# A hybrid decoder layer on one core: order and place of the two weight parts, small lead products, and pooled sums and heads over more steps

## The chip, the cores and the metric

The kernel runs on one core of one Trainium2 chip. The metric is device time in microseconds (us) of one execution, the median of several. The core has five engines with instruction streams of their own: TensorE (PE, whose loads of stationary operands appear as PEld), VectorE (DVE), ScalarE (ACT), GpSimd (POOL) and SyncE (SP), which here only issues DMA transfers. Each engine works through its instructions in program order and waits on semaphores for the others.

## The reference

One layer on 256 tokens of width 2048, all in float32, cut to what matters:

```
h    = rms_norm(x, attn_norm_g)
proj = h @ w_in                                  # 2048 x 4096
q, k, v, p = split(proj, [1024, 2048, 3072])
q, k = rms_norm(heads(q), q_norm_g), rms_norm(heads(k), k_norm_g)   # 8 heads of 128
a = softmax(q k^T / sqrt(128) + rel_bias, causal) @ v
# pooling mixer: 4 groups of 256 channels, windows 2, 4, 8, 16
m = concat_g((window_sum_g(p_g) / count_g - p_g) @ pool_w[g]) * pool_scale
x = x + concat(a, m) @ w_out                     # 2048 x 2048
u = rms_norm(x, ffn_norm_g) @ w_up               # 2048 x 11264
y = conv_b + causal depthwise convolution of u, width 3
gate, val = split(y, 2)
x = x + (silu(gate) * val) @ w_down              # 5632 x 2048
```

The block-sparse selection of the attention has one block of 256 tokens here, so that it is plain causal attention.

## The kernel before

**Two parts for one float32.** TensorE multiplies in a format of fewer bits (fp32r). So each weight and each activation is split into a high part, the rounded value, and a low part, the rest. A product is the sum of three: high by high, low weight by high activation, high weight by low activation. ScalarE writes the high part of a weight chunk `wh` (L115, a copy with rounding), VectorE the low part `wl` (L116, raw minus high).

**Chunks and steps.** The weights come as 88 chunks of 128 x 2048 floats in the order of use. A step is half a chunk, 1024 columns; there are 176. SP loads chunk after chunk into four raw buffers; `release` issues the next load as soon as a raw buffer has been split. `wh` and `wl` have three buffers each, rows of 2048 + 64 floats, and the chunk begins some floats into the row: `WOFF` gives that offset for high and low, one pair for the first 24 chunks and one for all others. The tiles of the activations (`xh`, `cat`, `x2h`, `hid`) hold per row, for each of 16 blocks of channels, 256 tokens of the high part and then 256 of the low part.

**The two kinds of product.** In the first 48 steps the activations are the stationary operand (loaded, 128 x 128) and 512 columns of weights stream past it: the v projection (L152, 16 steps, accumulated in four 512-column banks) and the q and k projections (L162, four blocks of eight steps, in the order k, q, k, q, four heads each). In all later steps the weights are loaded and the activations stream. There `feat_mm` issues two products per block of 128 x 128 weights: `wl` with the 256 columns of the high activations (L169), then `wh` with all 512 columns, high and low (L171). Both add into a 512-column bank of PSUM, whose two halves are added up when the block is done (`add_halves`, ScalarE L400 and VectorE L401). Two places use `feat_sum` (L178), with three products of 256 columns and no sum behind: the products of the pooling mixer (`pool_half`) and the last down block.

**The order of the steps.** v (steps 0 to 15); k, q, k, q (16 to 47); the pooling mixer's projection for g = 3, 2, 1, 0 (48 to 63, four steps each); the output projection, eight blocks of 256 output channels (four steps each, with two steps of `pool_half` among those of the first); then three times: a stretch of the gate and value blocks in turn, and eight down blocks. What the other engines do in between is set by hand: `after(u, f)` hangs f behind step u, and the loop at the end (L655 to L666) runs, for each step: the split of the chunk that is used two chunks later (at even steps), what was deferred, the products of the step, and the hooks. So a hook's place in each engine's stream is fixed by its step.

**Attention.** When a q or k block is done, `head_norm` normalises it by head (VectorE writes `qn` or `kn`), and two steps later `head_T` transposes it on TensorE (L338). Per head, `scores` multiplies, adds the bias, finds the row maxima and writes their negatives (`mx`, L358) on VectorE and takes the exponential on ScalarE (L360); `normalise` (one step later) takes the reciprocal of the sums and scales `e` on VectorE (L365, L367); `probs_T` (three steps later) transposes `e` on TensorE (L374); `head_out` (five steps later) multiplies by v (L384) and splits the result into `cat` (L390). A head starts every second step. The rows of the relative bias are written out to DRAM (`band`) and read back shifted as `T`, by the queue of POOL, once for each four heads.

**The pooling mixer.** Behind the last step of a group, `pool_window` adds the halves, scales (L407), sums the window by doubling (L411, one addition of 128 x 512 for each power of two: four for the window of 16, one for the window of 2), takes the mean (L413) and subtracts the input (L414). Two steps later (at once for g = 0) `pool_mixed` splits the result into `cat`.

**Behind an output block**, `residual` adds x and sums the squares for the second norm, and `x2_split` splits two blocks of channels into `x2h`, for the gate and value blocks. `stats2` (two steps into the first gate block) forms the row sums on TensorE (L281) for the scale that `gate` and `value` apply.

The lines that set pace and order:

```
WOFF = ((24, 24), (8, 24))
...
for n, (ws, k) in enumerate(ks):
    nc.tensor.matmul(ps[:, S:], wl[:, ws], act[:, k, 0, :], start=(first and n == 0), ...)
    nc.tensor.matmul(ps, wh[:, ws], act[:, k, :, :], start=False, ...)
...
after(u, lambda h=h, b=b: scores(h, st["qT", b], st["kT", b], st["T", b]))
after(u + 1, lambda h=h: normalise(h))
after(u + 3, lambda h=h: probs_T(h))
after(u + 5, lambda h=h: head_out(h))
```

Of the kernel before, what the change touches and what calls it, by code (L numbers as in the profile page):

```python
# [34 lines left out]
NH = 8  # L35
# [16 lines left out]
WOFF = ((24, 24), (8, 24))  # L52
# [19 lines left out]
def layer(ctx: ExitStack, tc: tile.TileContext, xT, wts, par, relT, ident_d, onehot_d, icnt_d, out):  # L72
# [27 lines left out]
    def load(c, pieces=1, j=0, queue=None):  # L100

        if c not in raws:
            raws[c] = wpool.tile([P, CH], F32, name="raw", tag="raw", bufs=RAWS)
        s = slice(j * CH // pieces, (j + 1) * CH // pieces)
        (queue or nc.sync).dma_start(raws[c][:, s], wts[c][:, s])
# [35 lines left out]
    def val_half(u, ps):  # L141
# [5 lines left out]
        for b in (0, 1) if u < KT - 2 else (u - KT + 2,):  # L147
            for k, (wh, wl) in zip(ks, parts):
                for t in range(NT):
                    ws, ts = slice(b * 512, (b + 1) * 512), slice(t * P, (t + 1) * P)  # L150
                    for n, (a, w) in enumerate(((0, wh), (0, wl), (1, wh))):
                        nc.tensor.matmul(ps[b][:, t, :], xh[:, k, a, ts], w[:, ws],  # L152
                                         start=(k == 0 and n == 0), stop=(k == KT - 1 and n == 2))
# [12 lines left out]
    def feat_mm(ps, wh, wl, act, ks, first, last):  # L166

        for n, (ws, k) in enumerate(ks):
            nc.tensor.matmul(ps[:, S:], wl[:, ws], act[:, k, 0, :],  # L169
                             start=(first and n == 0), stop=False, skip_group_check=True)  # L170
            nc.tensor.matmul(ps, wh[:, ws], act[:, k, :, :], start=False,  # L171
# [46 lines left out]
    load(0, 4, 0, nc.scalar)  # L218
    nc.scalar.preload_act_table_set("natural_log_exp_and_others")
    load_xT(0, 1)  # L220
    load(0, 4, 1)
    load_xT(1, 2)
    load(0, 2, 1)
    for c in range(1, RAWS):
        load_xT(2 * c, 2 * c + 2)
        load(c, 2, 0)
        load(c, 2, 1)
    x_first()
    split_piece(0, 0, 512)
    split_piece(0, 512, 512)  # L230
# [6 lines left out]
    rsb = early.tile([NH, L], F32, name="rsb", tag="e", bufs=2)  # L237
# [108 lines left out]
    def scores(h, qT, kT, T):  # L346
# [6 lines left out]
        e = early.tile([P, L], F32, name="e", tag="e", bufs=2)  # L353
        mx = early.tile([P, 4], F32, name="mx", tag="mx", bufs=2)
# [48 lines left out]
    def pool_window(ps, g):  # L403
        s = early.tile([P, 2, S], F32, name="pst", tag=("sq", "hn")[g % 2])
        eng = nc.vector
        add_halves(s, ps)
        eng.tensor_tensor(pa[0][:, :, PAD:], s, rrow[:, None, :].to_broadcast([P, 2, S]), op=OP.mult)  # L407
        cur, d, i = pa[0], 1, 1
        while d < WINDOWS[g]:
            nxt = pa[i]  # L410
            eng.tensor_tensor(nxt[:, :, PAD:], cur[:, :, PAD:], cur[:, :, PAD - d:PAD + S - d], op=OP.add)  # L411
            cur, d, i = nxt, 2 * d, 3 - i
        eng.tensor_tensor(s, cur[:, :, PAD:], icnt[:, g:g + 1, :].to_broadcast([P, 2, S]), op=OP.mult)  # L413
        eng.tensor_tensor(s, s, pa[0][:, :, PAD:], op=OP.subtract)  # L414
        st["win", g] = s

# [316 lines left out]
```

## Time and profile before

| | us |
|---|---|
| runs: median of 3 (lowest, highest) | 1054.22 (1051.92, 1055.24) |
| the profiled execution, its own time | 1056.07 |
| its span, first to last instruction | 1054.3 |
| TensorE busy | 1036.8 (98%) |
| loads of its stationary operands | 900.1 (85%) |
| VectorE busy | 703.6 (67%) |
| ScalarE busy | 508.7 (48%) |

The profile's page comes from one execution with the hardware profiler. The span leaves out what lies before the first and behind the last instruction. Busy times are sums over an engine's instructions. TensorE's products overlap in its pipeline, and their ends are modelled, so the length of a product in a row is longer than the step to the next one; the pace has to be read from starts. The mean clock granted to TensorE over the span was 0.994 of full speed. The DMA engines moved 200.42 MB at 190 GB/s in the mean, and the main queue (the weights) kept them busy for 52.5% of the span.

By stretches, from the view of windows (us from the start of the span; busy times of the engines; TensorE's clock):

| stretch | steps in it | TensorE | VectorE | ScalarE | clock |
|---|---|---|---|---|---|
| 0 to 58 | v | 54.97 | 37.15 | 34.87 | 1.00 |
| 58 to 172 | k, q, k, q with the first heads | 109.52 | 61.77 | 48.95 | 0.97 |
| 172 to 214 | pooling mixer with the last heads | 37.39 | 33.41 | 18.12 | 0.96 |
| 214 to 324 | output projection | 108.47 | 76.45 | 58.39 | 1.00 |
| 324 to 1054 | gate, value, down | 726.41 | 494.84 | 348.36 | 1.00 |

In rows of the timeline the first column is the start and the second the length (of several instructions, from the first's start to the last's end); what stands in brackets is the idle time of the engine before the row and what ended it. In rows of the windows the columns are: the window, its length, busy time and count of PE, PEld, DVE, ACT and POOL, TensorE's granted clock, the share of the DMA engines, and GB/s.

### The profile page before, as it was taken

Reading aid. Unit: us, or ns where it says so; the run is one execution under the profiler, and the core shown is the slowest. Engines: PE = TensorE matmul, PEld = TensorE weight load, DVE = VectorE, ACT = ScalarE, POOL = GpSimd, SP = SyncE. Lnnn points to the kernel's source line nnn. Section 1 sums busy time; section 2 is a strip of 40 time slices with the busy share of each in tenths; the row PEclk is TensorE's granted clock in tenths of the full one; section 3 lists DMA queues with packets and bytes.
Section 4 is the critical chain, followed back from the end, with each engine's and each line's share of the span. In section 5 each row is a group of like instructions: output and inputs, shape, how many; then the busy total and the mean of one; then the engine's idle time right before and its main releaser. Section 6 shows DMA issues by size and latency. Waiting matters only on the chain.

```text
span 1054.3 us, 13723 instructions
## 1 busy us (share of the span) xinstructions
PE 1036.8 (98%) x5786; PEld 900.1 (85%) x5786; DVE 703.6 (67%) x755; ACT 508.7 (48%) x526; POOL 3.7 (0%) x13
## 2 busy tenths in 40 slices
PE   8999989899999999999999999999999999999998
PEld 7877778798887888888888888888888888888887
DVE  6654647786766777777655577776765557777763
ACT  7534543545545455455443454555543445555441
POOL 0000000000000000000000000000000000000000
PEclk9999989999999999999999999999999999999999
DMA  9677533456463555545555555455455554554551
GB/s 358 252 186 225 207 140 122 142 221 234 170 220 136 197 197 175 204 181 200 200 190 174 196 186 196 178 197 202 165 198 196 200 184 176 200 200 163 205 192 40
DMA packets 31102, 200.42 MB, mean 190 GB/s; under 512 B 3784, under 2 KB 4584, under 8 KB 8256
## 3 DMA queue, kind: packets, MB, share of 16 engines
q1 hardware_dynamic: 29904, 196.66, 52.5%
q0 software_dynamic: 992, 2.63, 1.5%
q8 instruction: 45, 0.74, 0.3%
q10 hardware_dynamic: 144, 0.26, 0.1%
q14 instruction: 17, 0.14, 0.0%
HBM read 195.86 MB, written 3.67 MB: 189 GB/s over the span
## 4 chain that ended last, share of the span: by engine, by line
PE 83%; DVE 3%; ACT 2%; issue 1%; ACTq 0%; DVEq 0%
PE ps_feat L171 53%; PE ps_feat L169 27%; PE ps_tok L162 2%; DVE wl L116 1%; PE ps_feat L178 1%; ACT wh L115 1%; ACT e L360 1%; PE ps_pool L178 1%; DVE pa L411 0%; PE ps_T L338 0%; DVE e L356 0%; PE ps_av L384 0%; DVE pst L413 0%; DVE pst L401 0%; DVE pa L407 0%
## 5 line engine op out<-in xcount | busy, mean ns | idle before, releaser
L116 DVE TENSOR_TENSOR wl<-raw,wh 128x2048 fp32r<-128x2048 f32 (+2 forms) x186 | 415.5, 2234 | 218.3 <-ACT wh L115 215.8
L171 PE MATMUL ps_feat<-x2h,wh 128*128 128x512 f32 x1408 | 489.8, 393 | 0.0
L115 ACT ACTIVATE wh<-raw 128x2048 fp32r<-128x2048 f32 (+2 forms) x186 | 346.7, 1864 | 102.2 <-PE ps_feat L171 61.9
L169 PE MATMUL ps_feat<-x2h,wl 128*128 128x256 f32 x1408 | 392.3, 279 | 0.0
L171 PEld LDWEIGHTS ps_feat<-x2h,wh 128*128 128x128 f32 x1408 | 264.9, 188 | 59.9
L169 PEld LDWEIGHTS ps_feat<-x2h,wl 128*128 128x128 f32 x1408 | 265.0, 188 | 0.0
L171 PE MATMUL ps_feat<-hid,wh 128*128 128x512 f32 x680 | 235.9, 392 | 0.0
L169 PE MATMUL ps_feat<-hid,wl 128*128 128x256 f32 x680 | 189.0, 278 | 0.0
L171 PEld LDWEIGHTS ps_feat<-hid,wh 128*128 128x128 f32 x680 | 127.6, 188 | 28.8
L169 PEld LDWEIGHTS ps_feat<-hid,wl 128*128 128x128 f32 x680 | 127.6, 188 | 0.0
L400 ACT ACTIVATE fs<-ps_feat 128x512 f32<-128x512 f32 x75 | 44.8, 597 | 170.8 <-PE ps_feat L171 170.8
L401 DVE TENSOR_TENSOR fs<-ps_feat,fs 128x512 f32<-128x512 f32 x75 | 51.7, 689 | 57.5 <-ACT fs L400 57.5
L171 PE MATMUL ps_feat<-cat,wh 128*128 128x512 f32 x256 | 88.9, 391 | 0.0
L162 PE MATMUL ps_tok<-wh,xh 128*128 128x512 f32 x256 | 85.5, 407 | 0.0
L169 PE MATMUL ps_feat<-cat,wl 128*128 128x256 f32 x256 | 71.5, 279 | 0.0
L162 PEld LDWEIGHTS ps_tok<-wh,xh 128*128 128x128 f32 x256 | 49.1, 192 | 11.8 <-issue 0.4
L171 PEld LDWEIGHTS ps_feat<-cat,wh 128*128 128x128 f32 x256 | 48.1, 188 | 10.5
L624 ACT ACTIVATE hid<-y 128x512 fp32r<-128x512 f32 x22 | 13.9, 633 | 86.7 <-DVE y L623 86.7
L162 PE MATMUL ps_tok<-wl,xh 128*128 128x512 f32 x128 | 51.4, 401 | 0.0
L169 PEld LDWEIGHTS ps_feat<-cat,wl 128*128 128x128 f32 x256 | 47.9, 187 | 0.2 <-DVE wl L116 0.2
L599 ACT ACTIVATE y<-u,pv 128x256 f32<-128x256 f32 x88 | 47.8, 591 | 0.0
L611 ACT ACTIVATE y<-y 128x512 f32<-128x512 f32 x22 | 13.9, 634 | 68.1 <-DVE y L602 68.1
(111 smaller groups left out, 680.9 us busy)
## 6 DMA issues: line engine op xcount, KB each, us to landing
raw<-in_wts SPq DMA_DIRECT2D x177, 1024.0 KB, 4.8
raw<-in_wts SPq DMA_DIRECT2D x7, 512.0 KB, 8.0
x<-in_xT SPq DMA_DIRECT2D x1, 2048.0 KB, 10.7
xboth<-in_xT SPq DMA_DIRECT2D x7, 256.0 KB, 8.7
out<-x SPq DMA_DIRECT2D x7, 256.0 KB, 3.3
band<-rsb POOLq DMA_DIRECT2D x1, 1536.0 KB, 35.1
T<-band POOLq DMA_DIRECT2D x2, 512.0 KB, 7.1
icnt<-in_icnt SPq DMA_DIRECT2D x1, 512.0 KB, 6.0
```

Of the source, the lines that this page charges most:

```text
L115: nc.scalar.activation(wh, w, AF.Copy)
L116: nc.vector.tensor_tensor(wl, w, wh.bitcast(F32), op=OP.subtract)
L162: nc.tensor.matmul(ps[:, t, :], act[:, k0 + k, a, ts], w[:, ws], start=(first and k == 0 and n == 0), stop=(last and k == 1 and n == 2))
L169: nc.tensor.matmul(ps[:, S:], wl[:, ws], act[:, k, 0, :], start=(first and n == 0), stop=False, skip_group_check=True)
L171: nc.tensor.matmul(ps, wh[:, ws], act[:, k, :, :], start=False, stop=(last and n == len(ks) - 1), skip_group_check=True)
L178: nc.tensor.matmul(ps, w[:, ws], act[:, k, a, :], start=(first and n == 0 and i == 0), stop=(last and n == len(ks) - 1 and i == 2))
L360: nc.scalar.activation(e[:, s], e[:, s], AF.Exp, bias=mx[:, t:t + 1], accum_out=mx[:, 2 + t:3 + t])
L400: nc.scalar.activation(dst, ps[:, :, S:], AF.Copy)
L401: nc.vector.tensor_tensor(dst, ps[:, :, :S], dst, op=OP.add)
L599: nc.scalar.activation(y[:, m, :], u[:, m, 2:], AF.Identity, scale=cw[2], bias=col(C_CB + f))
L611: nc.scalar.activation(y, y, AF.Silu)
L624: nc.scalar.activation(hid[:, ks, 0, :], y, AF.Copy)
```

## The change

**WOFF.** From chunk 24 on the low part begins 28 floats into its row instead of 24 (112 bytes instead of 96); the high part stays at 8 floats (32 bytes).

**feat_mm** issues the product of `wh` (512 columns) first and that of `wl` (256 columns) behind it.

**A lead product** of 16 columns, with `wh` loaded and 16 columns of `wl` streaming, into the first bank of a block, which the block's first product then overwrites. It stands ahead of seven blocks: the output block g = 1, and in each third the first gate block and the first down block.

**The first chunk** is loaded, split and used in pieces of 256, 256 and 512 columns (`FIRST`) instead of 512 and 512 in its first half; `load` takes a start and a length.

**Heads.** `head_T` moves from two to three steps behind its block; the heads start four steps behind the end of their q block instead of three, with `normalise` one step, `probs_T` four and `head_out` six steps behind `scores`. `e` and `mx` have three buffers instead of two. The second `T` is fetched at `at + 8`, with `at` one step later.

**Pooled sums.** `pool_window` keeps the sum of the halves and the scaling. `window_sums` does two of the doublings behind the same step, and two more with the mean (`window_mean`) one step later; `pool_mixed` stays two steps later. For g = 0 all stays behind the last step.

**x2_split** of the last output block moves from a hook behind the first gate step into the end of the block's own last step.

```diff
-WOFF = ((24, 24), (8, 24))
+WOFF = ((24, 24), (8, 28))
...
-        for b in (0, 1) if u < KT - 2 else (u - KT + 2,):
+        if u == 0:
+            pieces = FIRST
+        else:
+            pieces = ((0, 512), (512, 512)) if u < KT - 2 else (((u - KT + 2) * 512, 512),)
+        for lo, cols in pieces:
...
         for n, (ws, k) in enumerate(ks):
-            nc.tensor.matmul(ps[:, S:], wl[:, ws], act[:, k, 0, :],
+            nc.tensor.matmul(ps, wh[:, ws], act[:, k, :, :],
                              start=(first and n == 0), stop=False, skip_group_check=True)
-            nc.tensor.matmul(ps, wh[:, ws], act[:, k, :, :], start=False,
+            nc.tensor.matmul(ps[:, S:], wl[:, ws], act[:, k, 0, :], start=False,
                              stop=(last and n == len(ks) - 1), skip_group_check=True)
...
-    load(0, 4, 0, nc.scalar)
+    FIRST = ((0, 256), (256, 256), (512, 512))
+    load(0, *FIRST[0], queue=nc.scalar)
     nc.scalar.preload_act_table_set("natural_log_exp_and_others")
     load_xT(0, 1)
-    load(0, 4, 1)
+    for piece in FIRST[1:]:
+        load(0, *piece)
     load_xT(1, 2)
-    load(0, 2, 1)
+    load(0, HALF, HALF)
...
-        e = early.tile([P, L], F32, name="e", tag="e", bufs=2)
-        mx = early.tile([P, 4], F32, name="mx", tag="mx", bufs=2)
+        e = early.tile([P, L], F32, name="e", tag="e", bufs=3)
+        mx = early.tile([P, 4], F32, name="mx", tag="mx", bufs=3)
...
+    def window_sums(g, d, n):
+
+        for _ in range(n):
+            if d == WINDOWS[g]:
+                return
+            i = d.bit_length()
+            cur, nxt = pa[0 if d == 1 else 1 + i % 2], pa[1 + (i + 1) % 2]
+            nc.vector.tensor_tensor(nxt[:, :, PAD:], cur[:, :, PAD:], cur[:, :, PAD - d:PAD + S - d], op=OP.add)
+            d *= 2
+
+    def window_mean(g):
+        s = st["win", g]
+        cur = pa[1 + WINDOWS[g].bit_length() % 2]
+        nc.vector.tensor_tensor(s, cur[:, :, PAD:], icnt[:, g:g + 1, :].to_broadcast([P, 2, S]), op=OP.mult)
+        nc.vector.tensor_tensor(s, s, pa[0][:, :, PAD:], op=OP.subtract)
...
+                    if lead:
+                        wh, wl = wparts[u // 2]
+                        o = (u % 2) * HALF
+                        nc.tensor.matmul(box["ps"][0][:, :16], wh[:, o:o + P], wl[:, o:o + 16], start=True, stop=True)
...
-        after(len(steps) + (2 if g else 0), lambda g=g: pool_mixed(g))
+        e = len(steps)
+        if g:
+            after(e, lambda g=g: window_sums(g, 1, 2))
+            after(e + 1, lambda g=g: (window_sums(g, 4, 2), window_mean(g)))
+            after(e + 2, lambda g=g: pool_mixed(g))
+        else:
+            after(e, lambda g=g: (window_sums(g, 1, 1), window_mean(g), pool_mixed(g)))
...
-            after(st[nm, b, "end"] + 2, lambda nm=nm, b=b, gc=gc: st.__setitem__(
+            after(st[nm, b, "end"] + 3, lambda nm=nm, b=b, gc=gc: st.__setitem__(
                 (nm + "T", b), head_T(st[nm, b], gc, nm + "T")))
-        at = st["q", b, "end"] + 3
+        at = st["q", b, "end"] + 4
...
-            after(u + 3, lambda h=h: probs_T(h))
-            after(u + 5, lambda h=h: head_out(h))
+            after(u + 4, lambda h=h: probs_T(h))
+            after(u + 6, lambda h=h: head_out(h))
         if b == 0:
-            after(at + 7, lambda: st.__setitem__(("T", 1), bias_tile(4)))
+            after(at + 8, lambda: st.__setitem__(("T", 1), bias_tile(4)))
...
+        def post(ps, g=g):
+            residual(ps, g)
+            if g == D // 256 - 1:
+                x2_split(g)
+        steps += feat_block(lambda: st["cat"], OK, post, lead=(g == 1))
+        if g < D // 256 - 1:
+            after(len(steps) + (2 if g == 0 else 0), lambda g=g: x2_split(g))
...
+            steps += feat_block(lambda: late["h"], XK, lambda ps, g=g: gate(ps, g), lead=(g == g0))
...
+                                     lambda ps, g=g, n=n, final=final: down(ps, g, n == 2, final), final,
+                                     lead=(g == 0)))
```

TensorE at the border between the last output block (streaming `cat`) and the first gate block (streaming `x2h`), before:

```order
L171 MATMUL ps_feat<-cat,wh 128x512
L169 MATMUL ps_feat<-cat,wl 128x256
L171 MATMUL ps_feat<-cat,wh 128x512
L169 MATMUL ps_feat<-x2h,wl 128x256
L171 MATMUL ps_feat<-x2h,wh 128x512
L169 MATMUL ps_feat<-x2h,wl 128x256
```

and now:

```order
L177 MATMUL ps_feat<-cat,wl 128x256
L175 MATMUL ps_feat<-cat,wh 128x512
L177 MATMUL ps_feat<-cat,wl 128x256
L489 MATMUL ps_feat<-wl,wh 128x16
L175 MATMUL ps_feat<-x2h,wh 128x512
L177 MATMUL ps_feat<-x2h,wl 128x256
```

Low and high have changed places in each pair, and the lead product L489 stands between the blocks. Loads and products still alternate: the load of the `wl` of L177 runs beside the 512 columns of L175, that of the next `wh` beside the 256 columns of L177.

VectorE at the second of the last four heads (in the first pooling group; L356 finds the row maxima, `mx` holds their negatives), before:

```order
L356 ISA e,mx<-ps_s,T 128x128
L356 ISA mx 128x1
L356 ISA e,mx<-ps_s,T 128x256
L356 ISA mx 128x1
L358 TENSOR_SCALAR mx<-mx 128x2
L365 RECIPROCAL mx<-mx 128x2
L367 SCALAR_TENSOR_TENSOR e<-e,mx,rrow 128x128
L367 SCALAR_TENSOR_TENSOR e<-e,mx,rrow 128x256
L116 TENSOR_TENSOR wl<-raw,wh 128x2048
```

and now (L364 is the L356 of before, L366 the L358, L373 and L375 the L365 and L367, L438 `pool_mixed`):

```order
L364 ISA e,mx<-ps_s,T 128x128
L364 ISA mx 128x1
L364 ISA e,mx<-ps_s,T 128x256
L364 ISA mx 128x1
L366 TENSOR_SCALAR mx<-mx 128x2
L116 TENSOR_TENSOR wl<-raw,wh 128x2048
L438 TENSOR_TENSOR cat<-pst,cat 128x2x256
L373 RECIPROCAL mx<-mx 128x2
L375 SCALAR_TENSOR_TENSOR e<-e,mx,rrow 128x128
L375 SCALAR_TENSOR_TENSOR e<-e,mx,rrow 128x256
```

The heads have moved by one step, so that the split of the next chunk, which runs at even steps, now stands between the maxima and the normalisation instead of behind it; the mixer's split L438 follows it there.

More of the change, by code (lines that the diff above doesn't have):

```diff
@@ L98, in layer, with load @@
     raws, wparts = {}, {}
-    def load(c, pieces=1, j=0, queue=None):
+    def load(c, lo=0, n=CH, queue=None):
         if c not in raws:
             raws[c] = wpool.tile([P, CH], F32, name="raw", tag="raw", bufs=RAWS)
-        s = slice(j * CH // pieces, (j + 1) * CH // pieces)
+        s = slice(lo, lo + n)
         (queue or nc.sync).dma_start(raws[c][:, s], wts[c][:, s])
@@ L216, in x_first @@
         nc.vector.scalar_tensor_tensor(lo, xin[:, 0, :], xboth[:, :1], hi.bitcast(F32), op0=OP.mult, op1=OP.subtract)
-    load(0, 4, 0, nc.scalar)
+    FIRST = ((0, 256), (256, 256), (512, 512))
+    load(0, *FIRST[0], queue=nc.scalar)
     nc.scalar.preload_act_table_set("natural_log_exp_and_others")
     load_xT(0, 1)
-    load(0, 4, 1)
+    for piece in FIRST[1:]:
+        load(0, *piece)
     load_xT(1, 2)
-    load(0, 2, 1)
+    load(0, HALF, HALF)
     for c in range(1, RAWS):
         load_xT(2 * c, 2 * c + 2)
-        load(c, 2, 0)
-        load(c, 2, 1)
+        load(c, 0, HALF)
+        load(c, HALF, HALF)
     x_first()
-    split_piece(0, 0, 512)
-    split_piece(0, 512, 512)
+    for piece in FIRST:
+        split_piece(0, *piece)
     for k in range(1, AHEAD):
@@ L236, in layer @@
     onehot = early.tile([32, 2 * S], F32, name="onehot", tag="T")
-    rsb = early.tile([NH, L], F32, name="rsb", tag="e", bufs=2)
+    rsb = early.tile([NH, L], F32, name="rsb", tag="e", bufs=3)
     icnt = early.tile([P, 4, S], F32, name="icnt")
@@ L460, in tok_block, with feat_block @@
             steps.append([run])
-    def feat_block(act, ks, post, final=False):
+    def feat_block(act, ks, post, final=False, lead=False):
         box, runs = {}, []
@@ L574, in layer @@
     for g in range(D // 256):
-        steps += feat_block(lambda: st["cat"], OK, lambda ps, g=g: residual(ps, g))
-        after(len(steps) + (2 if g == 0 else 0), lambda g=g: x2_split(g))
+        def post(ps, g=g):
[5 more added lines that the diff above has]
+            after(len(steps) + (2 if g == 0 else 0), lambda g=g: x2_split(g))
         if g == 0:
@@ L641, in layer @@
         for g in range(g0, g1):
-            steps += feat_block(lambda: late["h"], XK, lambda ps, g=g: gate(ps, g))
+            steps += feat_block(lambda: late["h"], XK, lambda ps, g=g: gate(ps, g), lead=(g == g0))
             steps += feat_block(lambda: late["h"], XK, lambda ps, g=g, j=g - g0: value(ps, g, j))
```

19 lines of the change are left out of this document (6 added, 13 removed).

## The prediction

> **What bounds the kernel now.** I read the page's busy times first, then TensorE's own waits, then its timeline. The page gives TensorE 98% of the span, and its waits are few:
>
> ```profile
> PE 1036.8 (98%) x5786; PEld 900.1 (85%) x5786; DVE 703.6 (67%) x755; ACT 508.7 (48%) x526; POOL 3.7 (0%) x13
> ...
> PE ps_av L384 <- DVE mx L365: 3.1, 1, 3.1
> PE ps_T L338 <- DVE cat L390: 3.0, 1, 3.0
> PE ps_row L281 <- issue: 2.0, 1, 2.0
> PE ps_T L338 <- DVE qn L329: 1.5, 1, 1.5
> PE ps_eT L374 <- DVE e L367: 1.5, 1, 1.5
> ```
>
> The timeline gives the places of the first, the last of attention's, and the one of L281 (the bracket holds the idle time before):
>
> ```profile
> 107.04 1.09 PE L338 MATMUL ps_T<-ident,qn 128*128 128x128 f32 x8 [1.47 <-DVE qn L329]
> 198.24 0.67 PE L384 MATMUL ps_av<-eT,v 128*128 128x256 f32 x2 [3.08 <-DVE mx L365]
> 324.47 0.67 PE L281 MATMUL ps_row<-sq,ones 128*128 128x256 f32 x2 [2.00 <-issue]
> ```
>
> Four of the five stand between 105 and 198 us, where attention and the pooling mixer share VectorE. The list of waits holds none that ends behind 324 us. Behind three of the waits the windows show TensorE at half clock:
>
> ```profile
> 137.40:144.30 6.90, 5.90 (x18) 5.04 (x19) 2.19 (x5) 3.77 (x6) 0.04 (x1) 0.51 0.57 217
> 198.90:202.30 3.40, 3.40 (x15) 3.01 (x14) 2.97 (x7) 0.30 (x1) 0.00 (x0) 0.50 0.14 19
> 325.20:328.60 3.40, 3.40 (x12) 2.89 (x11) 1.68 (x4) 0.83 (x2) 0.00 (x0) 0.50 0.81 306
> ```
>
> Half of the work time in them is lost: about 2.9 (5.90 / 2), 1.7 and 1.7 us. So 11.1 us of waits and 6.3 us of half clock can be had from scheduling, 17.4 us in all. Everything else is the pace of the products, and this is its size:
>
> ```profile
> L171 PE MATMUL ps_feat<-x2h,wh 128*128 128x512 f32 x1408 | 489.8, 393 | 0.0
> L171 PE MATMUL ps_feat<-hid,wh 128*128 128x512 f32 x680 | 235.9, 392 | 0.0
> L171 PE MATMUL ps_feat<-cat,wh 128*128 128x512 f32 x256 | 88.9, 391 | 0.0
> ```
>
> Each of these high products has a low one of 256 columns (L169) beside it: 1408 + 680 + 256 = 2344 pairs. The timeline shows their pace at full clock, and at half clock (326 us):
>
> ```profile
> 340.08 0.28 PE L169 MATMUL ps_feat<-x2h,wl 128*128 128x256 f32 x1
> 340.19 0.39 PE L171 MATMUL ps_feat<-x2h,wh 128*128 128x512 f32 x1
> 340.42 0.28 PE L169 MATMUL ps_feat<-x2h,wl 128*128 128x256 f32 x1
> ...
> 326.10 0.41 PE L169 MATMUL ps_feat<-x2h,wl 128*128 128x256 f32 x1
> 326.31 0.63 PE L171 MATMUL ps_feat<-x2h,wh 128*128 128x512 f32 x1
> 326.74 0.41 PE L169 MATMUL ps_feat<-x2h,wl 128*128 128x256 f32 x1
> ```
>
> The first column is the start, so what counts is the step from row to row. A more exact period comes from ScalarE, which repeats its split once per gate and value block (64 pairs):
>
> ```profile
> 348.49 1.90 ACT L115 ACTIVATE wh<-raw 128x2048 fp32r<-128x2048 f32 x1
> 481.61 1.90 ACT L115 ACTIVATE wh<-raw 128x2048 fp32r<-128x2048 f32 x1
> ```
>
> Six such blocks, 384 pairs, take 133.12 us: 346.7 ns per pair, so 2344 pairs are 812.6 us of the 1054. At half clock the pair takes 0.64 us, and half of that is 320 ns. At full clock 26.7 ns are lost in each pair, 13.3 per product, though nobody is waited for. Two other stages, of equal products, show what the loss can be:
>
> ```profile
> 73.98 0.63 PE L162 MATMUL ps_tok<-wh,xh 128*128 128x512 f32 x2
> 74.45 0.40 PE L162 MATMUL ps_tok<-wl,xh 128*128 128x512 f32 x1
> 74.68 0.63 PE L162 MATMUL ps_tok<-wh,xh 128*128 128x512 f32 x2
> ...
> 222.14 0.40 PE L178 MATMUL ps_pool<-cat,wh 128*128 128x256 f32 x2
> 222.38 0.28 PE L178 MATMUL ps_pool<-cat,wl 128*128 128x256 f32 x1
> 222.50 0.40 PE L178 MATMUL ps_pool<-cat,wh 128*128 128x256 f32 x2
> ```
>
> L162: three products of 512 columns in 0.70 us, 233.3 each against 213.3 by the half clock: 20.0 lost. L178: three of 256 in 0.36 us, 120.0 against 106.7: 13.3 lost. So the loss comes in units of 6.7 ns: two per product where the columns stream from the activations (L178, L171 with L169), three where they stream from the weights (L162). If length alone set it, a 512 with a 256 would lose 33.3; it loses 26.7. What differs is which row of SBUF is loaded while which is streamed.
>
> **The change part by part.** *Low part moved by 16 bytes (WOFF).* In the code each piece that is loaded or streamed starts a multiple of 512 bytes into its row, so one offset fixes the relation between a load and the columns streaming past it for all 2344 pairs. So far the offsets are 96 and 32 bytes; the low part's load, which runs beside the 512 columns of L171, goes to 112, an odd multiple of 16. No row shows an odd one, so the price is bounded by the losses above: at best the low load costs nothing, −13.3 ns × 2344 = −31.3 us; at worst it takes a unit more, as in L162, +6.7 × 2344 = +15.6 us. I take one unit less, −15.6 us: the loss moves in units, the offset moves by the smallest step that can change the relation, and L162 against L178 (one unit apart) is the nearest pair of rows.
>
> The Trainium skill speaks against it: TensorE: Matmul & The Clock Gate, Step-by-step: what each phase is for, says that loads and streamed columns have independent SBUF read ports, so that loading the next weights takes nothing from the running product. By it this term is 0 wherever the weights lie. The trace agrees only at half clock; at full clock 13.3 to 20.0 ns per product are lost.
>
> *High part first (L171 before L169).* Loads and products alternate as before, so the steady pace has no term. At a block's start the low part is needed one product later; TensorE waits for no low part after 11 us, so nothing is won.
>
> *The 16-column products.* Seven more loads and products on a TensorE that is never idle there. The nearest row has one column:
>
> ```profile
> 57.91 0.50 PE L301 MATMUL ps_col<-ones,xboth 128*128 128x1 f32 x4
> 58.27 0.68 PE L281 MATMUL ps_row<-xboth,ones 128*128 128x256 f32 x2
> ```
>
> Four in 0.36 us are 0.09 each; with L178's 0.12 as the other end, 7 × 0.1 = +0.7 us (0.6 to 0.8).
>
> *Smaller first pieces.* TensorE's second half step and SP's issues set the pace at the start:
>
> ```profile
> 8.07 1.06 ACT L115 ACTIVATE wh<-raw 128x1024 fp32r<-128x1024 f32 x1 [1.50 <-DMA raw<-in_wts]
> 10.45 0.50 PE L152 MATMUL ps_val<-wl,xh 128*128 128x512 f32 x1 [0.76 <-DVE wl L116]
> ...
> 3.07 1.17 SPq L105 DMA_DIRECT2D raw<-in_wts  x2
> ```
>
> That half is a transfer that the change puts one SP issue further back (two take 1.17 us, one 0.6). The first product comes earlier, but the wait at 10.45 absorbs it: 0 to +0.6, taken as +0.1.
>
> *Heads one step later, pooled sums over three steps.* A step is some 2.8 us (12 × 0.233, 8 × 0.347). The wait for qn (1.5) should go, since 2.8 is more than 1.5. The others hang on VectorE, and there the new order costs something. One head, now:
>
> ```profile
> 184.05 0.17 DVE L358 TENSOR_SCALAR mx<-mx 128x2 f32<-128x2 f32 x1
> 185.28 0.17 DVE L365 RECIPROCAL mx<-mx 128x2 f32<-128x2 f32 x1 [1.05 <-ACT e L360]
> 185.48 0.75 DVE L367 SCALAR_TENSOR_TENSOR e<-e,mx,rrow 128x128 f32<-128x128 f32 x2
> 187.46 2.29 DVE L116 TENSOR_TENSOR wl<-raw,wh 128x2048 fp32r<-128x2048 f32 x1 [1.23 <-ACT wh L115]
> ...
> 185.52 1.91 ACT L115 ACTIVATE wh<-raw 128x2048 fp32r<-128x2048 f32 x1
> ...
> 172.00:214.00 42.00, 37.39 (x209) 32.36 (x209) 33.41 (x64) 18.12 (x33) 0.00 (x0) 0.96 0.36 127
> ```
>
> After mx VectorE waits 1.05 for ScalarE's exponentials, normalises, and waits 1.23 for the high split: 2.3 us idle. In the new order the low split stands right behind mx; its high split on ScalarE still follows the exponentials (about 1.0, then 1.9), so VectorE idles 2.9 us in one stretch and normalises afterwards. Behind the waiting split stand the window sums and the normalisation, and TensorE's transposes wait for those. In 172 to 214 us VectorE works 33.4 of 42; with four heads at 2.9 us of waiting it would need 45.0, up to 3 us more than now. Against it: the wait of 1.5 goes, and the 3.0 before ps_T shrinks by 2.8, less 0.6 × 3 heads. That is −1.5 − 1.0 + 3 = about 0; the ends are −13.7 (the four waits' 9.1 and two half-clock windows' 4.6 all gone) and +5 (0.6 for each of eight heads). The T load (POOL queue) moves with its step and keeps eight steps of cover, and the third e buffer keeps a later head off one still to be transposed.
>
> *x2_split of the last group.* It passes one split on ScalarE and VectorE, but the sum L570, for which ps_row waits, still stands behind the same two low splits. 0; the 2.0 us and their half clock stay.
>
> Sum: −15.6 + 0.7 + 0.1 + 0 = −14.8 us. The profiled execution took 1056.07 us, 1.77 outside its span of 1054.3; it would take 1041.3. It lies 1.85 above the median of the runs shown (1054.22), and for that median the sum gives **1039 us**.
>
> **The rivals.**
> *The 16 bytes do nothing* (an independent port, or a loss that hangs on the count of loads alone). For it: L178 loses the same 13.3 per product as L171 with L169, though there the loads beside one product come from the high and the low tile in turn. Against it: L162. Time: 1054.2 + 0.8 = 1055, with the attention stage's ends 1041 to 1060.
> *The low load then costs nothing*: 1054.2 − 31.3 + 0.8 = 1024.
> *One unit more* (slower): the odd line meets the 512 streamed columns as the loads of L162 do, +15.6 + 0.8: 1071. It decides from about 0.35 ns per pair on, since 2344 pairs make 0.8 us of that; for it speaks that offsets of this kind lose three units in one stage already.
>
> **How the numbers follow.** One unit less 0.42 (1031 to 1047 with the attention stage's play); free 0.13; nothing 0.30; one unit more 0.15. A measurement of this kernel tells some 0.3% (3.2 us) from no change. Of the case "nothing" I put 0.20 within that, 0.06 faster through the stage, 0.04 slower: faster 0.42 + 0.13 + 0.06 = 0.61, same 0.20, slower 0.15 + 0.04 = 0.19. The range 1021 to 1058 holds the first, most of the free case and the third, about 0.82; it leaves out the last.
>
> **What would show it.** Right: 64 pairs in 21.76 us instead of 22.19 (340.0 ns a pair), steady to the end, L171's step near 223. Wrong in the main term: the period still at 346.7, or at 353.3. For the stage: waits before 224 us of some 7 to 12 us in all, VectorE waiting 2.9 us behind each mx, the qn wait gone, ps_row's 2.0 still there. The prediction fails altogether if the pace changes between stages, since I let one pace hold for all 2344 pairs.

## The result and the profile after

The changed kernel takes **1062.9 us** (median of 4 runs, 1062.08 to 1063.29) against 1054.47 before: ratio 1.0083, interval 1.0065 to 1.0101. It is slower by 0.8%, where 1.4% faster was forecast, and lies above the forecast's range. The profiled execution took 1063.29 us with a span of 1061.5, 7.2 more than before.

Two counts have to be put right first: the kernel has 181 chunks and 362 steps, not 88 and 176, and 2472 pairs of products, since the 128 pairs of the pooling projection (L171 with `xh`) were left out of the 2344.

The page's busy times and TensorE's waits (total, times, longest), after:

```profile
PE 1042.3 (98%) x5799; PEld 901.3 (85%) x5799; DVE 702.7 (66%) x756; ACT 507.7 (48%) x527; POOL 3.7 (0%) x13
...
PE ps_av L392 <- DVE cat L398: 4.2, 2, 3.5
PE ps_val L157 <- ACT wh L115: 2.1, 1, 2.1
PE ps_s L359 <- DVE mx L364: 2.0, 2, 1.2
PE ps_T L346 <- DVE cat L398: 2.0, 1, 2.0
PE ps_row L289 <- issue: 1.9, 1, 1.9
```

Where the time went, by the starts of each stage's first product in the two traces (us):

| stretch | before | after | difference |
|---|---|---|---|
| to the end of v | 52.31 | 56.58 | +4.27 |
| k, q, k, q | 108.14 | 103.70 | −4.44 |
| pooling projection | 58.92 | 60.87 | +1.96 |
| output projection | 94.62 | 96.62 | +2.00 |
| gate, value, down (to the end of the span) | 740.3 | 743.7 | +3.4 |

**The start.** The timeline of TensorE and ScalarE and the windows of the first microseconds, after (columns as before):

```profile
11.05 0.79 PE L157 MATMUL ps_val<-wh,xh 128*128 128x512 f32 x1 [2.15 <-ACT wh L115]
...
9.94 1.06 ACT L115 ACTIVATE wh<-raw 128x1024 fp32r<-128x1024 f32 x1 [2.40 <-DMA raw<-in_wts]
...
4.00:5.00 1.00, 0.86 (x5) 0.49 (x4) 0.96 (x3) 0.72 (x2) 0.00 (x0) 1.00 0.66 197
5.00:6.00 1.00, 0.76 (x7) 0.74 (x7) 0.54 (x2) 0.00 (x0) 0.00 (x0) 1.00 0.70 208
...
10.70:17.55 6.85, 6.04 (x13) 4.42 (x14) 5.58 (x7) 5.50 (x9) 0.00 (x0) 0.51 1.03 413
```

and the same two windows before:

```profile
4.00:5.00 1.00, 0.64 (x4) 0.45 (x3) 0.28 (x1) 0.12 (x1) 0.00 (x0) 1.00 1.00 339
5.00:6.00 1.00, 0.43 (x1) 0.19 (x1) 0.96 (x3) 0.97 (x2) 0.00 (x0) 1.00 1.07 327
```

With the smaller pieces the transfers run at 197 and 208 GB/s where they ran at 339 and 327. The second half of the first chunk is there for its split at 9.94 us instead of 8.07; TensorE waits for 2.15 us, and then runs at a clock of 0.51 for 6.85 us, in which half of its 6.04 us of work, about 3.0 us, is lost.

**The pace.** ScalarE's splits 12 chunks (192 pairs) apart, in the second gate and value stretch, after:

```profile
600.43 1.91 ACT L115 ACTIVATE wh<-raw 128x2048 fp32r<-128x2048 f32 x1
667.42 1.91 ACT L115 ACTIVATE wh<-raw 128x2048 fp32r<-128x2048 f32 x1
```

66.99 / 192 = 348.9 ns a pair, 2.2 more than before, and it is so from the first pair to the last. The starts of the high products stand 346, 349 and 352 ns apart in turn (rounded, 1046.67 in three pairs), where before they stood evenly 346.67 apart. 2472 x 2.22 = 5.5 us.

**The pooling mixer.** VectorE at one head, and two of TensorE's waits, after:

```profile
186.12 0.17 DVE L366 TENSOR_SCALAR mx<-mx 128x2 f32<-128x2 f32 x1
189.16 2.29 DVE L116 TENSOR_TENSOR wl<-raw,wh 128x2048 fp32r<-128x2048 f32 x1 [2.86 <-ACT wh L115]
191.36 0.68 DVE L438 TENSOR_TENSOR cat<-pst,cat 128x512 fp32r<-128x512 f32 x1
191.97 0.16 DVE L373 RECIPROCAL mx<-mx 128x2 f32<-128x2 f32 x1
...
194.84 0.92 PE L359 MATMUL ps_s<-kT,qT 128*128 128x128 f32 x4 [1.21 <-DVE mx L364]
204.87 0.70 PE L392 MATMUL ps_av<-eT,v 128*128 128x256 f32 x2 [3.52 <-DVE cat L398]
```

VectorE waits for 2.9 us behind the maxima, as forecast, and the chain behind it reaches TensorE's products of the next head (1.21) and of `head_out` (3.52).

### The profile page after: what moved, and what is told of

Read it like the earlier page. It is cut to its first block, busy times and chain, and to the rows that moved or that the text cites. A ratio compares the mean times of both kernels' runs of the same rounds, so it can differ in the third digit from the quotient of the medians.

```text
span 1061.5 us, 13820 instructions
## 1 busy us (share of the span) xinstructions
PE 1042.3 (98%) x5799; PEld 901.3 (85%) x5799; DVE 702.7 (66%) x756; ACT 507.7 (48%) x527; POOL 3.7 (0%) x13
## 4 chain that ended last, share of the span: by engine, by line
PE 86%; DVE 5%; DMA 4%; ACT 3%; issue 1%; SPq 0%; ACTq 0%; DVEq 0%
PE ps_feat L175 51%; PE ps_feat L177 26%; PE ps_val L157 4%; PE ps_tok L168 3%; DMA raw<-in_wts 3%; DVE wl L116 3%; ACT wh L115 2%; DMA x<-in_xT 1%; PE ps_feat L184 1%; ACT e L368 1%; DVE e L375 0%; DVE pa L425 0%; DVE e L364 0%; PE ps_av L392 0%; DVE pst L431 0%
## 5 line engine op out<-in xcount | busy, mean ns | idle before, releaser
L175 PE MATMUL ps_feat<-x2h,wh 128*128 128x512 f32 x1408 | 491.8, 393 | 0.0
L177 PE MATMUL ps_feat<-x2h,wl 128*128 128x256 f32 x1408 | 393.3, 279 | 0.0
L175 PEld LDWEIGHTS ps_feat<-x2h,wh 128*128 128x128 f32 x1408 | 264.6, 188 | 61.3
L177 PEld LDWEIGHTS ps_feat<-x2h,wl 128*128 128x128 f32 x1408 | 264.0, 187 | 0.0
L175 PE MATMUL ps_feat<-hid,wh 128*128 128x512 f32 x680 | 237.6, 393 | 0.0
L177 PE MATMUL ps_feat<-hid,wl 128*128 128x256 f32 x680 | 189.9, 279 | 0.0
L175 PEld LDWEIGHTS ps_feat<-hid,wh 128*128 128x128 f32 x680 | 127.8, 188 | 29.6
L177 PEld LDWEIGHTS ps_feat<-hid,wl 128*128 128x128 f32 x680 | 127.5, 187 | 0.0
L409 DVE TENSOR_TENSOR fs<-ps_feat,fs 128x512 f32<-128x512 f32 x75 | 51.6, 689 | 60.9 <-ACT fs L408 60.9
L175 PE MATMUL ps_feat<-cat,wh 128*128 128x512 f32 x256 | 89.9, 394 | 0.0
L177 PE MATMUL ps_feat<-cat,wl 128*128 128x256 f32 x256 | 71.6, 280 | 0.7 <-DVE wl L116 0.7
L175 PEld LDWEIGHTS ps_feat<-cat,wh 128*128 128x128 f32 x256 | 48.1, 188 | 11.3 <-DVE cat L462 0.3
L177 PEld LDWEIGHTS ps_feat<-cat,wl 128*128 128x128 f32 x256 | 48.0, 187 | 1.0 <-DVE wl L116 1.0
L175 PE MATMUL ps_feat<-xh,wh 128*128 128x512 f32 x128 | 47.2, 409 | 0.0
```

Source lines behind the costliest of these rows:

```text
L175: nc.tensor.matmul(ps, wh[:, ws], act[:, k, :, :], start=(first and n == 0), stop=False, skip_group_check=True)
L409: nc.vector.tensor_tensor(dst, ps[:, :, :S], dst, op=OP.add)
```

## The experiments

Ratios are to the kernel before on the same chip, intervals 95%. A place (16, 4) means the high part at 16 floats and the low part at 4. Executions at that place fall into two groups more than 20 us apart, so all times are given where both groups occur.

### The first pieces

```diff
-    FIRST = ((0, 256), (256, 256), (512, 512))
+    FIRST = ((0, 512), (512, 512))
```

> The changed kernel with the first half chunk loaded, split and used in two pieces of 512 columns, as before. In the changed kernel TensorE waits 2.15 us at 8.9 us for the high split of the second half step, and runs at half clock from 10.7 to 17.6 us; the v stage takes 51.95 us instead of 46.75, though it starts 0.93 earlier. Theory A (the smaller transfers slow the loads behind them, the wait grows past the point where the clock is halved): the wait falls back to under 1 us, no half clock, v stage near 46.8, the run 4.3 us faster than the changed kernel, near 1058.6. Theory B (half clock at the start comes by chance from execution to execution, whatever the pieces): v stage still 50 to 52, the run near 1062.9.

1060.6 us (5 runs), ratio 1.0054 (1.0042 to 1.0066): 2.3 less than the changed kernel by the medians, and about 3 by the two ratios, each to the kernel before on its own chip. TensorE's waits at the start of its timeline:

```profile
5.70 0.50 PE L157 MATMUL ps_val<-wh,xh 128*128 128x512 f32 x1 [1.09 <-ACT wh L115]
10.29 0.50 PE L157 MATMUL ps_val<-wl,xh 128*128 128x512 f32 x1 [0.76 <-DVE wl L116]
```

The wait of 2.15 and the half clock are gone, and v takes 46.47 instead of 51.95: theory A, by mechanism. The 4.3 forecast did not come in full: in this execution the half clock stands behind the wait for the row sums again (325 to 328.5 us, 1.7 lost), where the profiled execution of the changed kernel had none. Nor do the pieces decide alone: both profiled executions with the smaller pieces have half clock at the start, but so has one of the 18 with the old ones (the run with fifteen leads below, 3.4 us of it behind waits of 0.89 and 0.76 us). In the other run with the smaller pieces (place undone) the transfers ran at 236 and 274 GB/s and the wait was 1.55 us, so the size of this loss differs between executions.

### Place alone, place undone

```diff
-WOFF = ((24, 24), (8, 24))          # kernel before
+WOFF = ((24, 24), (8, 28))
```

> The kernel before with the low part at 28 floats instead of 24, and nothing else. In the changed kernel the pair takes 348.9 ns instead of 346.7. Theory O (the place of the low part sets the pace): 348.9 ns a pair here, and 2472 x 2.2 ns = 5.4 us more than before, near 1059.9. Theory R (high first sets the pace): 346.7 ns, near 1054.5. Theory L (the lead products put the pairs out of step): 346.7 ns, 1054.5.

```diff
-WOFF = ((24, 24), (8, 28))          # changed kernel
+WOFF = ((24, 24), (8, 24))
```

> The changed kernel with the low part back at 24 floats. Theory O: 346.7 ns a pair, 5.4 us faster than the changed kernel, near 1057.5. Theories R and L: 348.9 ns, near 1062.9. If place and order act only together, both this and the offset alone run at 346.7.

The place alone: 1059.56 us, ratio 1.0044 (1.0030 to 1.0059). ScalarE's splits 192 pairs apart:

```profile
603.98 1.90 ACT L115 ACTIVATE wh<-raw 128x2048 fp32r<-128x2048 f32 x1
670.97 1.90 ACT L115 ACTIVATE wh<-raw 128x2048 fp32r<-128x2048 f32 x1
```

66.99 again: 348.9. Undone in the changed kernel: 1058.95 us, ratio 1.0037 (1.0024 to 1.0050), 4.0 less than the changed kernel by the medians, and 4.9 by the ratios. Its splits 192 pairs apart:

```profile
603.90 1.90 ACT L115 ACTIVATE wh<-raw 128x2048 fp32r<-128x2048 f32 x1
670.47 1.90 ACT L115 ACTIVATE wh<-raw 128x2048 fp32r<-128x2048 f32 x1
```

66.57 / 192 = 346.7 ns a pair. Theory O; the place does it alone.

The kernel with the place undone, at the old pace, has the seven leads. A down block stretch with one lead in it takes 88.86 us instead of 88.75: 0.11 a lead, 0.8 us for all seven.

### Order alone, schedule alone

The kernel before with the two products of `feat_mm` exchanged, as in the change:

> The kernel before with the high product first in each pair, and nothing else. Theory O: 346.7 ns a pair, no change, 1055. Theory R: 348.9 ns or another period, 1058 to 1060 or more.

1055.46 us (11 runs), ratio 1.0004 (0.9995 to 1.0013), 346.67 ns a pair. The order costs nothing and brings nothing by itself.

The changed kernel with everything but the schedule taken back:

```diff
-WOFF = ((24, 24), (8, 28))
+WOFF = ((24, 24), (8, 24))
...
-    FIRST = ((0, 256), (256, 256), (512, 512))
+    FIRST = ((0, 512), (512, 512))
...
-                    if lead:
+                    if False:
```

and the low product first again.

> The changed kernel with the old places (8, 24), low first, no lead products and the old first pieces: what is left are the heads one step later, the pooled sums over more steps, and the last split of x2h in its block's own step. Theory S (the stage as read off the changed kernel): the waits of 1.5 and 1.1 before the transposes go, the half clock of 3.4 us lost at 137 us goes or moves, and VectorE's longer waits in the pooling mixer add 2 to 3.5 us: 1 to 4 us less than before, 1051 to 1054. Theory Z (the sum in the prediction): about 0, 1054 to 1056. If the half clock only moves, 1055 to 1057.

1055.33 us (11 runs), ratio 1.0005 (0.9995 to 1.0015): theory Z. The four q and k blocks take 3.7 us less than before, the pooling and output projections 3.8 more. Part of the 3.7 is half clock and not the schedule: the profiled execution before has 6.83 us of it at 137 us, this one 3.41, and in the run with the order alone, with none there, these blocks take 105.67 us against 104.44 here. What the transposes gain is given back where VectorE is late. The pooling projection takes 60.9 us in this run, with 6.83 us of half clock, and in that of the old first pieces, with none, where TensorE waits 2.29 us more for `head_out` (at 209.66 us): VectorE, and not TensorE's clock, sets its length. In the output projection TensorE waits 1.34 us at 247 us for a low part, where before it has no such wait.

### Two scans of the place

The kernel before, from chunk 49 on (gate, value, down) with another place for every four chunks; in the second scan with high first and another shuffle:

```diff
-            offs = WOFF[0 if c < TOK_CHUNKS else 1]
+            offs = WOFF[0 if c < TOK_CHUNKS else 1] if c < 49 else SCAN[(c - 49) // 4]
```

> The kernel before, with another place of the two parts for every four chunks (64 pairs, some 22 us) from the gate and value stage on: 32 places, high part at 0, 8, 16 or 24 floats, low part at 0, 4, 8 to 28, in a shuffled order. Same work. Theory O: the pair's period differs from place to place in units that repeat, with (8, 24) at 346.7 and (8, 28) at 348.9, and some places lower, down to 320 if a free one exists. Theory N (a loss of 13.3 ns per product belongs to the load itself, wherever it lies): 346 to 349 at every place, in no relation to the offsets.

> The kernel before with the high product first in each pair, and the same 32 places of the two parts as in the first scan, four chunks each, in another shuffled order. Theory O (place alone sets the pace): the same period at the same place as in the first scan: 340.0 at high 16, low 4; 346.7 at (8, 24); 348.9 at (8, 28); 353.3 at (8, 16), (16, 16) and (24, 16). Theory H (the pace is a phase into which TensorE falls after a change, and keeps): other periods at the same places, and 340.0 elsewhere or nowhere. Theory R (order and place act together): the table is another one, but a steady one.

The period in ns, from the starts of the high products in the trace, some 45 pairs for each place; where the scans differ by over 0.1, first / second. The stretches with TensorE's wait for the row sums in them ((24, 8) in the first scan, (24, 16) in the second) ran at 353.3 on both sides of the wait:

| high \ low | 0 | 4 | 8 | 12 | 16 | 20 | 24 | 28 |
|---|---|---|---|---|---|---|---|---|
| 0 | 351.1 | 353.3 | 351.1 | 353.3 / 346.7 | 346.7 / 353.3 | 349.3 | 346.7 | 346.7 |
| 8 | 346.7 | 353.3 | 350.0 | 350.0 / 353.3 | 353.3 | 348.9 | 346.7 | 348.9 |
| 16 | 346.7 | 340.0 / 351.1 | 349.3 | 346.7 | 353.3 | 346.7 | 348.9 | 353.3 / 340.0 |
| 24 | 348.9 / 346.7 | 350.0 | 353.3 | 346.7 | 353.3 | 346.7 | 346.7 | 346.7 |

26 of 32 places have one period in both scans, whatever the order and the place ahead of them: theory O holds for them, (8, 24) and (8, 28) among them. Six have two periods. At (16, 4) and (16, 28) runs below show several periods under one order of the products, as theory H says; for the other four the order, which also differed between the scans, is not ruled out (theory R). The unit less exists (340.0), and nothing goes below it.

### Place (16, 4) by itself

```diff
-WOFF = ((24, 24), (8, 24))
+WOFF = ((24, 24), (16, 4))
```

> The kernel before with the high part at 16 floats and the low part at 4 from chunk 24 on, the one place that ran at 340.0 ns a pair in the first scan, and nothing else. Theory O: 340.0 ns in all 2472 pairs, 6.67 less in each, 16.5 us less than before: near 1038.5. Theory H: it falls to 340.0 in some stages only, or in none: 1045 to 1055. Theory M (it holds only where x2h streams, as in the scan): 1408 pairs, 9.4 us less: near 1045.5.

Four executions: 1065.35, **1039.21**, 1064.06, 1065.45. The profiled one (1065.35) has its splits at

```profile
599.96 1.91 ACT L115 ACTIVATE wh<-raw 128x2048 fp32r<-128x2048 f32 x1
667.37 1.91 ACT L115 ACTIVATE wh<-raw 128x2048 fp32r<-128x2048 f32 x1
```

67.41 / 192 = 351.1. Ahead of 222 us, among TensorE's waits, some short stretches ran at 340.0 (the longest from 213 us); from 230 us on, and also behind the wait at 324, it was 351.1 to the end. None of the three theories had this: the place has two phases, and executions differ in which they keep.

### Leads of many lengths

The kernel before with high first and a lead product ahead of each block from the output projection on (75), its number of columns from a list:

```diff
+                    if not final and act() is not xh and leads:
+                        wh, wl = wparts[u // 2]
+                        o, c = (u % 2) * HALF, leads.pop(0)
+                        nc.tensor.matmul(box["ps"][0][:, :c], wh[:, o:o + P], wl[:, o:o + c], start=True, stop=True)
```

4 to 160 columns at (16, 4) and at the change's place (8, 28):

> The kernel before with high first, the parts at (16, 4), and a lead product ahead of each of 75 blocks of the output projection, gate, value and down, with 4, 8, 12 to 160 columns in turn and then in a shuffled order. Place (16, 4) alone ran at 340.0 ns a pair in one scan and in one execution, at 351.1 in the other scan and in most executions. Theory P (at this place the pair has two steady phases, and what comes between two pairs decides which): the period changes only at leads, between 340.0 and 351.1, and leads of the same length out of the same phase lead to the same one. Theory H2 (the phase is not set by single products but by stalls of 2 us and more): 351.1 or 340.0 throughout, whatever the leads. Time by P: between 1040 and 1066 with 75 x 0.11 = 8 us of leads on top.

> The same kernel and leads with the parts at the change's own places (8, 28), which ran at 348.9 ns a pair in six runs so far. Theory P: if this place too has a second phase, the period changes at some of the leads, to 340.0 or to another one; then the change's seven leads of 16 columns had a use and missed it. Theory O2 (one phase only at this place): 348.9 after every lead, some 1068 us in all (1060 and 8 of leads).

116 and 152 to 256 columns at (16, 4) and (16, 28):

> The kernel with 75 lead products at (16, 4) again, now with 116 and 152 to 256 columns, five times each in shuffled order. With short leads 11 of 75 blocks ran at 340.0, and both leads of 160 columns and the one of 152 gave it. Theory P1 (a lead's length alone decides the phase behind it): every length gives one period each time, 160 and 152 give 340.0 five times of five. Theory P2 (length and the phase before it, or the buffer in which the weights lie, decide together): some lengths give 340.0 more often than others, none always. Theory P3 (chance): each gives 340.0 in about 1 of 7.

> The same leads at (16, 28), which ran at 353.3 ns in the one scan and at 340.0 in the other. Theory P: two phases here too, 353.3 and 340.0, changing only at leads. Theory O2: one phase only, so that the order, which was the difference between the scans, decides: 340.0 throughout, as with high first in the scan, some 1048 us in all with the leads.

At (16, 4) the blocks run at 351.1 or 340.0, and behind the wait at 324 us the period changes at leads and nowhere else: behind 10 leads of 75 it is 340.0 with the short list (the 11 in the expectation for the long list is one too many), behind 11 with the long one (1069.19 and 1069.68 us). One length does not always lead to one period: 160 gave 340.0 in 5 of 7 cases in the two runs, 152 in 1 of 6: theory P, in the form P2. At (8, 28) the period is 348.9 behind each of the 75 leads (1069.72 us): one phase, theory O2. At (16, 28) it is 346.7 or 353.3, never the 340.0 of the scan (1065.44 us): a third phase, and the expectation missed it. There the length and the period ahead of the lead together fix the period behind it: no two of the 74 cases contradict each other.

### Can the fast phase be held?

Place (16, 4), leads of 160 columns ahead of each of 40 blocks, and two ahead of each of 35:

> Place (16, 4) with high first and a lead of 160 columns ahead of each of the first 40 blocks, two such leads ahead of each of the other 35. So far a lead of 160 gave 340.0 ns in 5 of 7 cases, each time from 351.1. Theory P2a (it leads to 340.0 from both phases in about 7 of 10 cases): some 28 of the first 40 blocks at 340.0, and more behind two leads; 1048 to 1054 us, 12 us of it leads. Theory P2b (from 340.0 it leads back): the two take turns, about half, 1056 to 1060. Theory P3 (chance): 1 of 7 blocks, near 1068.

Ahead of every fifth block only:

> The same with one lead of 160 columns ahead of every fifth block only, 15 in all: the phase that a lead gives should hold for five blocks (160 pairs). By P2a about 7 of 10 stretches at 340.0: mean 343.3 ns a pair, 7 us less than before and 1.7 us for the leads, near 1049. By P2b near 1055, by P3 near 1063.

Ahead of the first value block only:

> Place (16, 4), high first, and a single lead of 160 columns, ahead of the first value block (behind TensorE's wait for the row sums). In the run with a lead ahead of every block the lead at this place took the pair from 351.1 to 340.0 ns, and the next one, at the next block, back again. Theory T (each such lead turns the phase over, and without one it stays): 340.0 from 329 us to the end, some 2085 pairs, 13.9 us less than before, and 1.5 more for the 351.1 ahead of it: near 1042. Theory C (which phase follows is decided by something that differs from execution to execution): executions near 1042 and near 1063 by turns.

All blocks: 1072.36 us; in the first gate and value stretch the period goes to 340.0 and back at each lead, eight times over (P2b), and elsewhere it mostly stays at 351.1. Fifteen leads: 1065.36 us (4 runs, 1062.32 to 1067.29); the first gave 340.0, the second ended it. One lead: 1066.68, 1042.35, 1040.95, 1064.27, 1043.33: theory C. Leads of 160 columns end the fast phase more surely than they begin it.

Short leads, over the first 24 blocks, all of 16 columns, all of 12, and mixed:

```diff
+LEADS = [12, 24, 12, 44, 12, 8] * 4 + [0] * 51
```

> Place (16, 4), high first, leads of 16 columns ahead of the 24 blocks from the output projection to the last but one third of the first gate and value stretch (2.2 us of leads), none behind. In the runs with many lengths, leads of 8 to 44 columns left 340.0 ns as it was in 3 of 3 cases, and one of 16 took 351.1 to 340.0 in 1 of 2. Theory K (351.1 is a pattern over three pairs, so a lead of 16 hits it at one of three places, and 340.0 holds what it has): within a few blocks behind TensorE's wait at 324 us the period is 340.0 and stays, in every execution, near 1044. Theory C (the wait decides, leads do not): executions near 1042 and near 1066 by turns.

> The same with 12 columns in each lead. Theory K: as with 16, near 1044 in every execution. Theory C: executions near 1042 and near 1066 by turns.

> Place (16, 4), high first, 24 leads of 12, 24, 12, 44, 12 and 8 columns in turn, over the same blocks as in the two runs before. Leads of 12 left 340.0 as it was 21 times of 21, those of 8, 24 and 44 once of once; leads of one length were not enough to leave 351.1 in one execution each. Theory K2 (an execution stays at 351.1 where leads of one length meet its pattern at the same place again and again; other lengths between them break that): every execution near 1044. Theory C2 (what keeps it at 351.1 has nothing to do with the lengths): one execution in four or five near 1065 again.

16: 1066.61, 1044.92, 1044.33, 1043.68, 1043.34. 12: 1041.71, 1042.98, 1044.25, 1064.47. Mixed: **1042.34** (1041.63 to 1044.54, five of five), ratio **0.9877** (0.9858 to 0.9896), faster than both kernels. Its page, and ScalarE's splits 192 pairs apart:

```profile
PE 1025.4 (98%) x5810; PEld 895.6 (86%) x5810; DVE 702.9 (67%) x755; ACT 509.7 (49%) x526; POOL 3.7 (0%) x13
...
604.37 1.92 ACT L116 ACTIVATE wh<-raw 128x2048 fp32r<-128x2048 f32 x1
669.64 1.91 ACT L116 ACTIVATE wh<-raw 128x2048 fp32r<-128x2048 f32 x1
```

65.27 / 192 = 339.9 ns. In its profiled execution the first five leads left 351.1, the sixth (8 columns, at 281 us) began 340.0; TensorE's wait at 324 us ended it, and the second lead behind that (at 341 us) began it again, to the end. That mixed lengths do it in every execution is more than five executions show; leads of one length had failed in one of four and one of five.

The traces of seven runs with leads at (16, 4) (the two lists, the two runs with many leads of 160, and these three) also show what a lead does. At 351.1 the steps from one high product to the next are 353, 348 and 352 ns in turn, so a lead can come behind any of the three. Sorted by the last step ahead of the lead (leads right behind one of TensorE's long waits left out), the cases of a single lead in which 340.0 followed are:

| columns of the lead | from 351.1, behind the 352 step | from 351.1, behind the 348 or 353 step | from 340.0 |
|---|---|---|---|
| 160 | 12 of 12 | 0 of 38 | 0 of 9 |
| 116 | 3 of 3 | 0 of 4 | none tried |
| 16 | 3 of 3 | 0 of 16 | 4 of 5 |
| 12 | 4 of 4 | 0 of 3 | 28 of 28 |

In the one case of 16 columns that left 340.0, the step across the lead was 394 ns and not 367 or 368, so something else held TensorE there for some 27 ns. So it is not chance: the length of the lead and the place in the pattern decide together (theory P2). This also explains the execution of 1066.61 us with leads of 16: the 14 leads from 340 us on all came behind the 348 step, as theory K2 says, and none changed anything.

## Why the prediction was wrong

**What bounds the kernel** held: TensorE 98% busy, its pace the largest term. The working of the sum failed in two steps.

**The place of the low part**, forecast at −15.6 us, cost about +5.5 by the pair's period (4.2 and 4.0 by the medians of the two runs that put it in and took it out, 4.6 and 4.9 by their ratios). The step that failed: "I take one unit less, −15.6 us: the loss moves in units, the offset moves by the smallest step that can change the relation, and L162 against L178 (one unit apart) is the nearest pair of rows." Those rows differ in length and in which operand is loaded as well as in place; at most they say that places can differ, not in which direction this one does. The scans show that the nearest places of all carry no sign: beside (8, 24) at 346.7 stand (8, 20) and (8, 28) at 348.9, and (8, 16) at 353.3. The mean is not bound to the unit either, since a pattern can run over three pairs: 348.9 is a third of 6.7 above 346.7. The forecast's "one offset fixes the relation" holds for most places, and fails at the ones that matter: the unit less lies where there is more than one phase. That the term is not 0 wherever the weights lie is shown too: the place alone made the kernel 0.44% slower. By the rule of the Trainium skill (TensorE: Matmul & The Clock Gate, Step-by-step: what each phase is for), that loading takes nothing from a running product, it would have changed nothing; here the measurement decides against that rule.

**The smaller first pieces**, forecast at +0.1 with +0.6 as the end, cost 4.3 us in the profiled execution, and 2.3 by the medians or about 3 by the ratios of the run that took them back. The step: "The first product comes earlier, but the wait at 10.45 absorbs it: 0 to +0.6". It counted one more issue on SP and not what the transfers then carry: at 4 to 6 us they ran at about 200 instead of 330 GB/s (236 and 274 in the other run with these pieces). So the wait grew to 2.15 us (1.55 in the other), and half clock followed it, which the forecast had priced in the attention stage and not here.

By the ratios the parts come to 4.9 (place), about 3.1 (pieces), 0.8 (leads) and 0.5 (schedule), 9.3 us in all, where 0.83%, or 8.8 us, was measured.

**What held.** High first: nothing. The leads: 0.8 for 0.7. Heads and pooled sums: "about 0", measured 1.0005, by the terms given: the wait for `qn` is gone, the one before ps_T is 2.0 instead of 3.0, VectorE waits 2.9 us behind the maxima. The row sums' wait stays at 1.9. TensorE's longer waits behind the start come to about the same sum before and after (some 11 us); the half clock behind them moves from execution to execution. The schedule was thus rightly put at no gain.

**The rivals.** "The 16 bytes do nothing" (1055) lies 8 us below the result, the slower one (1071) 8 above; the slower one had the right sign, that the place costs, with the wrong size, a whole unit where a third was measured. The case of a free load finds no support: none of the 32 places ran near 320 ns. The range ended at 1058, because the slower case was left out of it and because no case joined a slower pace to a slower start.

**Open**: why a place has the period it has, and what decides which phase, and which point of its pattern, follows a long wait at (16, 4). What a lead does from there on is sorted out above from runs made for other questions; a run that sets the point on purpose was not made.

## What to carry to other kernels

Where TensorE never waits, measure the pace as starts over many equal products, and try places of the operands in one run, a few chunks each: two scans here told more than the forecast's argument from neighbouring rows. Repeat each place behind another neighbour, since a fast period that depends on what ran ahead of it can be lost at the next wait. A short product meant to move the pace should come in several lengths: one length can meet the same point of the pattern again and again. A smaller first piece brings the first product forward, and here slowed the transfers behind it; look at what the second wait becomes, and whether half clock follows.

## What the runs showed of the hardware

- The period of a pair of products with the same work ran from 340.0 to 353.3 ns. At 26 of 32 places it was the same in both scans, so it goes with where in their rows the two loaded parts begin. The values differ by 6.67 ns spread over one, two, three or more pairs (340.0, 346.7, 348.9, 349.3, 350.0, 351.1, 353.3).
- At (16, 4) the same instructions have two steady periods, at (16, 28) three; four more of the 32 places had two in the two scans, whose order of the products differed. A single product of 8 to 256 columns, or a wait, can change the phase; without either it held to the end. At (16, 4) a product of 160 columns turned 351.1 into 340.0 in 12 of 12 cases at one point of the three-pair pattern and in none of 38 at the other two.
- Waits of 1.55 us (place undone) and 2.15 us (after) at the start were followed by half clock for 3.4 and 6.8 us, and so were two of 0.89 and 0.76 us, 1.3 us apart (the run with fifteen leads); one of 1.09 us (old first pieces) was not. So the length of one wait does not decide it. Behind the row sums' wait of 1.9 to 2.0 us it came in some executions and not in others.
